# Down-projection weights of layer 1 on GpSimd's queue, two tiles ahead in four buffers, and the first tile's weight sums placed in the out-projection

## The chip, the cores and the metric

One core of one Trainium2 chip runs the whole program. Its engines are TensorE (PE, with its weight loads as PEld), VectorE (DVE, `V` in the code), ScalarE (ACT, `S`), GpSimd (POOL, `G`) and SyncE (SP), which here only issues DMAs. The metric is the device time of one execution in microseconds (us).

## The reference

A backbone block of two layers on 1024 latent tokens (and 256 context tokens) of width 1024. Layer 0 mixes by Fourier groups and windowed attention, layer 1 by neighbourhood attention; each layer ends with a SwiGLU feed-forward part of inner width 2816. The part that matters is layer 1's end:

```python
x = x + g1 * o                                     # o = mixer output @ w_out
h = _rms(x, norm2_g[i]) * (1.0 + sc2) + sh2
x = x + g2 * _swiglu(h, ffn_w_gate[i], ffn_w_up[i], ffn_w_down[i])

def _swiglu(h, wg, wu, wd):
    return (jax.nn.silu(h @ wg) * (h @ wu)) @ wd
```

All inputs are float32.

## The kernel before

Every float32 product is made of three matmuls on split operands: a number is hi + lo, hi its cast to the PE's float32 format, lo the rest, and hi·hi + lo·hi + hi·lo is summed in PSUM (`mm3`, L74 to L76; L76 is the last of a group). So each weight tile that arrives raw from memory must first be cast (ACT) and subtracted (DVE or POOL). `parts_of` does it for four 128x128 blocks at a time: the cast to w_hi at L1239, and the subtraction to w_lo at L1244, on POOL straight from w_hi, on DVE from a copy of w_hi in PSUM (`pmisc`, L1243).

Layer 1 ends with three loops. `out_proj1` runs once for each half (`ci` = 0, 1) of 512 tokens, over eight output tiles of 128 columns in falling order; it prepares the next tile's weights ahead, advances a norm's generator (`own`: `norm1s`) by one step and a second (`side`) by three. `norm1s` writes h in eight pieces of 128x512 (nrm_h). For the first half they go to `combine`, which makes the sums s_sum on POOL and splits them into c_hi and c_lo; the second half's pieces are stored to memory (h_d) and read back later as h_in.

Then, for each half, the feed-forward part walks 22 tiles (`NF`) of 128 inner columns. `gate_up1(f)` computes gate and up of tile f with a seven-product scheme for 2x2 block matrices: the gate and up weights (w_gate, w_up, 128x1024 each, loaded by SP at L1232 into a ring of four buffers w_raw) are the four blocks b11, b21, b12, b22, and POOL forms the sums t1 to t4 (L1328, L1329, L1333, L1337). `product7` makes one product p_ps of 12 matmuls 128x256; there are three PSUM buffers for these. ACT copies the first product to p (L1331), DVE adds the others up, ACT applies Silu, and act_hi (L1358) and act_lo (L1359) are the split result. The blocks b21 and b22 have their w_lo made on POOL, the other five on DVE.

`down_weights1(f)` loads tile f's down weights in two parts (wd_raw, 128x512, by SP at L1373, two buffers), casts them on ACT (L1374) and subtracts on POOL (L1375) into the "room": the buffers of the out-projection's inputs h_out[1], so both the hi and the lo parts are called h_hi or h_lo by the name of the buffer, depending on the pair. `down1` multiplies two tiles' results by their down weights: eight d_ps groups of six matmuls 128x512, each added to x by DVE (L1384). It runs for tiles f − 2 and f − 1 after the products of each even f, so the period of the loop is two tiles, called a pair below. The first four of the eight groups read the first part of each tile's room, the last four the second part.

A scheduler orders each engine's instructions from the program order and its own estimate of when they can run; the engines then keep that order, and each engine's queue is in order. That holds for SP's DMA issues too. Semaphores carry the waits between engines.

Of the kernel before, what the change touches and what calls it, by code (L numbers as in the profile page):

```python
# [9 lines left out]
F32 = mybir.dt.float32  # L10
F32R = mybir.dt.float32r
AF = mybir.ActivationFunctionType
ALU = mybir.AluOpType
# [3 lines left out]
P = 128  # L17
# [10 lines left out]
NF = DFF // P  # L28
# [35 lines left out]
def build(tc, io):  # L64
    nc = tc.nc
    V, S, G, TE = nc.vector, nc.scalar, nc.gpsimd, nc.tensor
    pools = Pools(tc)

    def fl(ap):
        return ap.bitcast(F32)  # L70

    def mm3(out, lh, ll, rh, rl, first, last):

        TE.matmul(out, lh, rh, start=first, stop=False)  # L74
        TE.matmul(out, lh, rl, start=False, stop=False)  # L75
        TE.matmul(out, ll, rh, start=False, stop=last)  # L76
# [35 lines left out]
    def vec(l, which):  # L112
        return mod[l][:, which * KT:(which + 1) * KT, :]
# [36 lines left out]
    def advance(steps, n):  # L150

        for _ in range(n):
            if next(steps, steps) is steps:
                return
# [35 lines left out]
    wk, wk_cm = pools.open("wk0", bufs=2, side="right")  # L190
# [158 lines left out]
    for c in range(T // CH):  # L349
        h_hi, h_lo = hs[c]  # L350

        for u in range(CH // P):
# [34 lines left out]
            for i, h0, nh in ((0, 0, 8), (1, 8, 2)):  # L387
                src = pqf[:, h0 * HD:(h0 + nh) * HD]
# [83 lines left out]
    for half in range(2):  # L472
# [5 lines left out]
        for gg in range(2):  # L478
# [3 lines left out]
            for i0, parts in ((0, (0, 4)), (2, (1, 2)), (4, (3,))):  # L482
# [8 lines left out]
                n = len(parts)  # L491
                src = ps[:, 0:n].rearrange("p n r l -> p r n l")
# [18 lines left out]
    g = fp.tile([P, 2, 512], F32, name="fg", tag="fa")  # L511
# [6 lines left out]
    for grp in range(4):  # L518
# [5 lines left out]
        src = ps.rearrange("p n r l -> p r n l")  # L524
# [699 lines left out]
    wk, wk_cm = pools.open("wk1")  # L1224
# [5 lines left out]
    def raw_weights(src):  # L1230
        raw = wr.tile([P, KT, P], F32, name="w_raw")
        nc.sync.dma_start(raw, src)  # L1232
        return raw

    def parts_of(src, eng=V):


        hi, lo = (ww.tile([P, 4, P], F32R, name=n) for n in ("w_hi", "w_lo"))
        S.copy(hi, src)  # L1239
        first = fl(hi)  # L1240
        if eng is V:
            first = ph.tile([P, 512], F32, name="pmisc").rearrange("p (k n) -> p k n", n=P)
            S.copy(first, fl(hi))  # L1243
        eng.tensor_tensor(lo, src, first, ALU.subtract)  # L1244
        return hi, lo

    def out_weights(dt):
        raw = raw_weights(io["w_out1"][dt])
        old = wr.tile([P, SEQ], F32, name="x_old", tag="w_raw")
        nc.sync.dma_start(old, x_d[:, dt])  # L1250
        return [parts_of(raw[:, i:i + 4]) for i in (0, 4)], old

    def out_proj1(ci, ready, own, side=iter(()), then=lambda: None):

        h_hi, h_lo = h_out[ci]
        for dt in reversed(range(KT)):
            ws, old = ready
            ready = out_weights(dt - 1) if dt else then()
            ps = pd.tile([P, 512], F32, name="d_ps")
            for k in range(KT):  # L1260
                hi, lo = ws[k // 4]
                mm3(ps, hi[:, k % 4], lo[:, k % 4], h_hi[:, k], h_lo[:, k], k == 0, k == KT - 1)
            cols = slice(ci * 32, ci * 32 + 32)
            V.scalar_tensor_tensor(x[:, dt, ci * 512:ci * 512 + 512].rearrange("p (c r) -> p c r", r=GH),
                                   ps.rearrange("p (c r) -> p c r", r=GH), vec(1, 2)[:, dt, 0:1],
                                   old.rearrange("p (r c) -> p r c", c=GW)[:, :, cols].rearrange("p r c -> p c r"),
                                   ALU.mult, ALU.add)
            advance(own, 1)
            advance(side, 3)
        return ready  # L1270

    def norm1s(ci, adder, done):


        ts = slice(ci * 512, ci * 512 + 512)
        ss = wk.tile([P, 512], F32, name="nrm_ss")
        for i, k in enumerate(reversed(range(KT))):
            if i == 0:
                S.activation(ss, x[:, k, ts], AF.Square)
            else:  # L1280
                sq = wk.tile([P, 512], F32, name="nrm_sq", tag="t", bufs=4)
                S.activation(sq, x[:, k, ts], AF.Square)
                adder.tensor_tensor(ss, ss, sq, ALU.add)
            yield
        for r in norm_rstd(ss, 512, wk, ph):
            yield
        for i in range(4):
            both = []
            for k in (i, i + 4):
                t = wk.tile([P, 512], F32, name="nrm_t", tag="t", bufs=4)  # L1290
                V.scalar_tensor_tensor(t, x[:, k, ts], nA[3][:, k, 0:1], r, ALU.mult, ALU.mult)
                h = wk.tile([P, 512], F32, name="nrm_h", bufs=2)
                S.activation(h, t, AF.Identity, bias=vec(1, 3)[:, k, 0:1], scale=1.0)
                both.append(h)
                yield
            done(i, *both)
            yield
# [19 lines left out]
            mm3(ps, w[0][:, k], w[1][:, k], c_hi[:, slot, k], c_lo[:, slot, k], k == 0, k == 3)  # L1317
        return ps

    def gate_up1(f, side=iter(())):  # L1320
        g, u = raw_weights(io["w_gate"][1, f]), raw_weights(io["w_up"][1, f])
        b11, b21, b12, b22 = g[:, 0:4], g[:, 4:8], u[:, 0:4], u[:, 4:8]
        t1, t2, t3, t4 = (wk.tile([P, 4, P], F32, name=n, tag="t", bufs=4) for n in ("t1", "t2", "t3", "t4"))
        p1, u2, u3, sg = (wk.tile([P, HT], F32, name=n) for n in ("p1", "u2", "u3", "sg"))
        av = wk.tile([P, 2, HT], F32, name="av", bufs=2)
        hi, lo = (wk.tile([P, 512], F32R, name=n, bufs=4) for n in ("act_hi", "act_lo"))
        w = parts_of(b11)
        G.tensor_tensor(t1, b12, b11, ALU.subtract)  # L1328
        G.tensor_tensor(t2, b22, t1, ALU.subtract)  # L1329
        ps = product7(w, 0)  # L1330
        S.copy(p1, ps)  # L1331
        w = parts_of(t2)
        G.tensor_tensor(t3, b22, b12, ALU.subtract)  # L1333
        ps = product7(w, 4)
        V.tensor_tensor(u2, ps, p1, ALU.add)
        w = parts_of(t3)
        G.tensor_tensor(t4, t2, b21, ALU.subtract)  # L1337
        ps = product7(w, 5)
        V.tensor_tensor(u3, ps, u2, ALU.add)
        w = parts_of(t1)  # L1340
        ps = product7(w, 3)
        V.tensor_tensor(av[:, 1], ps, u3, ALU.add)
        V.tensor_tensor(u2, ps, u2, ALU.add)
        w = parts_of(t4)
        ps = product7(w, 2)
        V.tensor_tensor(u3, u3, ps, ALU.subtract)
        S.activation(u3, u3, AF.Silu)
        w = parts_of(b21, G)
        ps = product7(w, 1)
        V.tensor_tensor(av[:, 1], av[:, 1], u3, ALU.mult)  # L1350
        V.tensor_tensor(sg, ps, p1, ALU.add)
        S.activation(sg, sg, AF.Silu)
        w = parts_of(b22, G)
        ps = product7(w, 6)
        V.tensor_tensor(u2, ps, u2, ALU.add)
        V.tensor_tensor(av[:, 0], u2, sg, ALU.mult)
        avf = av.rearrange("p a n -> p (a n)")
        S.copy(hi, avf)  # L1358
        V.tensor_tensor(lo, avf, fl(hi), ALU.subtract)  # L1359
        advance(side, 2)  # L1360
        return hi, lo
# [6 lines left out]
    def down_weights1(f):  # L1368

        w_in = w_room[f // 2 % 2]  # L1370
        for h in range(2):
            raw = wk.tile([P, 4, P], F32, name="wd_raw", bufs=2)
            nc.sync.dma_start(raw, io["w_down"][1, f][:, 4 * h:4 * h + 4])  # L1373
            S.copy(w_in[:, f % 2, h, 0], raw)  # L1374
            G.tensor_tensor(w_in[:, f % 2, h, 1], raw, fl(w_in[:, f % 2, h, 0]), ALU.subtract)  # L1375

# [16 lines left out]
    own0 = norm1s(0, G, combine)  # L1393
    ready = out_proj1(0, out_weights(KT - 1), own0, then=lambda: out_weights(KT - 1))
# [2 lines left out]
    c_hi = cc.tile([P, 7, 4, HT], F32R, name="c_hi")  # L1397
    c_lo = cc.tile([P, 7, 4, HT], F32R, name="c_lo")
    own1 = norm1s(1, V, keep)
    out_proj1(1, ready, own1, own0)  # L1400
    advance(own0, 99)
    for ci in range(2):
        acts = {}
        for f in range(NF):
            if f:
                down_weights1(f - 1)
            acts[f] = gate_up1(f, own1 if f else iter(()))
            if f % 2 == 0 and 2 <= f < NF - 2:
                down1(ci, (f - 2, f - 1), [acts.pop(f - 2), acts.pop(f - 1)], False)
        down_weights1(NF - 1)  # L1410

        h_in = []
        for i in range(4 if ci == 0 else 0):
            h_in.append(wr.tile([P, 2, 512], F32, name="h_in", tag="w_raw"))
            for n in range(2):
                nc.sync.dma_start(h_in[i][:, n], h_d[:, i + 4 * n])

        def amid(dt):
            if dt % 4 == 1 and h_in:
                h = h_in.pop(0)  # L1420
                combine(3 - len(h_in), h[:, 0], h[:, 1], tags=("t", "t"))

        for f in (NF - 4, NF - 2):
            down1(ci, (f, f + 1), [acts.pop(f), acts.pop(f + 1)], f == NF - 2, amid)
# [113 lines left out]
```

## Time and profile before

| | |
|---|---|
| runs | 3011.53, 3016.84, 3020.38 us; median 3016.84 |
| profiled execution | 3014.64 us; its span, first to last instruction, 3012.9 us |
| instructions | 44371 |
| mean granted TensorE clock | 0.976 |
| busy | PE 95%, PEld 79%, DVE 51%, ACT 40%, POOL 27% of the span |
| out-projection's end and feed-forward of layer 1 | from about 2195 us to the end, 3012.9 us |

In profile rows a time is followed by a duration, the engine and the line. "PE p_ps L74 <- ACT p L1331: 29.2, 8, 5.2" means that PE, about to run line 74, waited for the instruction of ACT at line 1331: 29.2 us in total, 8 times, 5.2 at most. In the rows of single instructions, a bracket at the end holds the idle time of the engine just before and what ended it; "x4" means four neighbouring instructions told as one row. "SPq" is SP issuing DMAs: a long duration there means that later issues of the row waited for buffers.

### The profile page before, as it was taken

Reading aid. Unit: us, or ns where it says so; the run is one execution under the profiler, and the core shown is the slowest. Engines: PE = TensorE matmul, PEld = TensorE weight load, DVE = VectorE, ACT = ScalarE, POOL = GpSimd, SP = SyncE. Lnnn points to the kernel's source line nnn. Section 1 sums busy time; section 2 is a strip of 40 time slices with the busy share of each in tenths; the row PEclk is TensorE's granted clock in tenths of the full one; section 3 lists DMA queues with packets and bytes.
Section 4 is the critical chain, followed back from the end, with each engine's and each line's share of the span. In section 5 each row is a group of like instructions: output and inputs, shape, how many; then the busy total and the mean of one; then the engine's idle time right before and its main releaser. Section 6 shows DMA issues by size and latency. Waiting matters only on the chain. (4 is left out here: it accounts for less than half of the span.)

```text
span 3012.9 us, 44371 instructions
## 1 busy us (share of the span) xinstructions
PE 2848.3 (95%) x16874; PEld 2383.4 (79%) x16874; DVE 1550.6 (51%) x3084; ACT 1200.7 (40%) x2390; POOL 809.7 (27%) x826
## 2 busy tenths in 40 slices
PE   7989999999999999999899999999989898889899
PEld 5876768888888888888767887777778888788888
DVE  5775553632323333333673343665566566755566
ACT  4445552411111111111452223666665555655553
POOL 0112322000000000000310003553266555755553
PEclk9989999999999999999999999999989999999999
DMA  7236563111111110110244338773533222422221
GB/s 271 101 99 244 211 227 116 49 43 49 36 35 35 43 39 32 42 42 30 74 128 121 99 102 203 177 172 93 168 120 121 91 85 85 140 85 85 85 85 64
DMA packets 137701, 310.59 MB, mean 103 GB/s; under 512 B 11504, under 2 KB 69360, under 8 KB 130448
## 3 DMA queue, kind: packets, MB, share of 16 engines
q1 hardware_dynamic: 129056, 288.80, 30.5%
q0 software_dynamic: 1952, 8.32, 1.0%
q10 hardware_dynamic: 6480, 10.63, 0.9%
q8 instruction: 134, 2.20, 0.3%
q14 instruction: 79, 0.65, 0.1%
HBM read 264.58 MB, written 43.12 MB: 102 GB/s over the span
## 5 line engine op out<-in xcount | busy, mean ns | idle before, releaser
L74 PE MATMUL p_ps<-c_hi,w_hi 128*128 128x256 f32 x1232 | 364.5, 296 | 75.9 <-ACT p L1331 58.1
L76 PE MATMUL p_ps<-c_hi,w_lo 128*128 128x256 f32 x1232 | 358.7, 292 | 6.6 <-DVE w_lo L1244 3.4
L75 PE MATMUL p_ps<-c_lo,w_hi 128*128 128x256 f32 x1232 | 358.7, 291 | 0.0
L74 PEld LDWEIGHTS p_ps<-c_hi,w_hi 128*128 128x128 f32 x1232 | 249.2, 202 | 84.5 <-ACT p L1331 62.5
L810 POOL TENSOR_TENSOR nrm_ss<-nrm_ss,nrm_sq 128x512 f32<-128x512 f32 (+1 forms) x31 | 39.3, 1269 | 1013.1 <-PE d_ps L76 935.7
L775 ACT CAST w_hi<-w_raw 128x1024 fp32r<-128x1024 f32 x106 | 110.2, 1049 | 482.5 <-PE d_ps L75 270.5
L76 PEld LDWEIGHTS p_ps<-c_hi,w_lo 128*128 128x128 f32 x1232 | 248.3, 202 | 8.1 <-DVE w_lo L1244 4.1
L75 PEld LDWEIGHTS p_ps<-c_lo,w_hi 128*128 128x128 f32 x1232 | 249.8, 203 | 0.9
L580 POOL TENSOR_SCALAR pr<-pr,st 128x640 f32<-128x640 f32 (+2 forms) x208 | 156.1, 751 | 267.2 <-DVE st L579 176.9
L878 DVE SCALAR_TENSOR_TENSOR x<-d_ps,mod,x 128x512 f32<-128x512 f32 (+1 forms) x240 | 157.6, 661 | 125.3 <-PE d_ps L76 125.3
L776 DVE TENSOR_TENSOR w_lo<-w_raw,w_hi 128x1024 fp32r<-128x1024 f32 x102 | 124.1, 1223 | 184.7 <-ACT w_hi L775 182.3
L862 DVE TENSOR_TENSOR sg<-sg,u_ps 128x512 f32<-128x512 f32 (+1 forms) x66 | 39.5, 599 | 320.0 <-PE u_ps L76 320.0
L74 PE MATMUL d_ps<-act_hi,w_hi 128*128 128x512 f32 (+1 forms) x528 | 189.3, 359 | 3.4 <-DVE x L878 3.4
L75 PE MATMUL d_ps<-act_lo,w_hi 128*128 128x512 f32 (+1 forms) x528 | 189.2, 358 | 1.3 <-DVE act_lo L864 1.3
L76 PE MATMUL d_ps<-act_hi,w_lo 128*128 128x512 f32 (+1 forms) x528 | 189.3, 358 | 0.0
L74 PE MATMUL u_ps<-o_hi,w_hi 128*128 128x512 f32 (+1 forms) x528 | 188.3, 357 | 0.0
L75 PE MATMUL u_ps<-o_lo,w_hi 128*128 128x512 f32 (+1 forms) x528 | 188.3, 357 | 0.0
L76 PE MATMUL u_ps<-o_hi,w_lo 128*128 128x512 f32 (+1 forms) x528 | 188.3, 357 | 0.0
L74 PE MATMUL g_ps<-o_hi,w_hi 128*128 128x512 f32 (+1 forms) x528 | 188.3, 357 | 0.0
L75 PE MATMUL g_ps<-o_lo,w_hi 128*128 128x512 f32 (+1 forms) x528 | 188.2, 357 | 0.0
L76 PE MATMUL g_ps<-o_hi,w_lo 128*128 128x512 f32 (+1 forms) x528 | 188.2, 357 | 0.0
L574 ACT ACTIVATE pr<-sm,st 128x640 f32<-128x640 f32 (+4 forms) x208 | 162.7, 782 | 31.1 <-POOL sm L563 22.3
(321 smaller groups left out, 7437.4 us busy)
## 6 DMA issues: line engine op xcount, KB each, us to landing
ada_w<-ada_w SPq DMA_DIRECT2D x48, 1024.0 KB, 4.9
w_raw<-w_gate SPq DMA_DIRECT2D x66, 512.0 KB, 3.5
w_raw<-w_up SPq DMA_DIRECT2D x66, 512.0 KB, 3.9
wd_raw<-w_down SPq DMA_DIRECT2D x88, 256.0 KB, 2.8
k<-k_d SPq DMA_DIRECT2D x28, 640.0 KB, 10.0
w_raw<-w_out SPq DMA_DIRECT2D x32, 512.0 KB, 3.6
w_raw<-w_in SPq DMA_DIRECT2D x24, 512.0 KB, 4.0
w_raw<-w_down SPq DMA_DIRECT2D x22, 512.0 KB, 3.5
```

Of the source, the lines that this page charges most:

```text
L74: TE.matmul(out, lh, rh, start=first, stop=False)
L75: TE.matmul(out, lh, rl, start=False, stop=False)
L76: TE.matmul(out, ll, rh, start=False, stop=last)
L574: S.activation(self.pr[:, :n], self.sm[:, :n], AF.Exp, bias=st[:, 0:1], scale=-1.0, accum_out=st[:, 1:2])
L580: G.tensor_scalar(self.pr[:, :n], self.pr[:, :n], st[:, 3:4], 0.0, ALU.mult, ALU.add)
L775: S.copy(hi, raw)
L776: eng.tensor_tensor(lo, raw, fl(hi), ALU.subtract)
L810: adder(i).tensor_tensor(ss, ss, sq, ALU.add)
L862: V.tensor_tensor(sg[:, :n], sg[:, :n], u_ps[:, :n], ALU.mult)
L878: V.scalar_tensor_tensor(xs, self.shaped(ps[:, :n]), vec(l, 5)[:, dt, v:v + 1], xs, ALU.mult, ALU.add)
```

## The change

Five things change. The down weights are loaded by GpSimd's queue instead of SP's, their ring has four buffers and shares them with nrm_h (which had two of its own), and `down_weights1` is called two tiles ahead of the tile's use in program order. `out_weights` passes `past=False`, so that DVE subtracts from w_hi itself and ACT's copy to PSUM is left out in the out-projection. The side generator goes two steps per tile instead of three. And the loads and the first two sums of the first feed-forward tile are called at the last tile of the second half's `out_proj1`.

```diff
@@ -1232,13 +1232,13 @@
         nc.sync.dma_start(raw, src)
         return raw
 
-    def parts_of(src, eng=V):
+    def parts_of(src, eng=V, past=True):
 
 
         hi, lo = (ww.tile([P, 4, P], F32R, name=n) for n in ("w_hi", "w_lo"))
         S.copy(hi, src)
         first = fl(hi)
-        if eng is V:
+        if eng is V and past:
             first = ph.tile([P, 512], F32, name="pmisc").rearrange("p (k n) -> p k n", n=P)
             S.copy(first, fl(hi))
         eng.tensor_tensor(lo, src, first, ALU.subtract)
@@ -1248,7 +1248,7 @@
         raw = raw_weights(io["w_out1"][dt])
         old = wr.tile([P, SEQ], F32, name="x_old", tag="w_raw")
         nc.sync.dma_start(old, x_d[:, dt])
-        return [parts_of(raw[:, i:i + 4]) for i in (0, 4)], old
+        return [parts_of(raw[:, i:i + 4], past=False) for i in (0, 4)], old
 
     def out_proj1(ci, ready, own, side=iter(()), then=lambda: None):
 
@@ -1266,7 +1266,7 @@
                                    old.rearrange("p (r c) -> p r c", c=GW)[:, :, cols].rearrange("p r c -> p c r"),
                                    ALU.mult, ALU.add)
             advance(own, 1)
-            advance(side, 3)
+            advance(side, 2)
         return ready
 
     def norm1s(ci, adder, done):
@@ -1289,7 +1289,7 @@
             for k in (i, i + 4):
                 t = wk.tile([P, 512], F32, name="nrm_t", tag="t", bufs=4)
                 V.scalar_tensor_tensor(t, x[:, k, ts], nA[3][:, k, 0:1], r, ALU.mult, ALU.mult)
-                h = wk.tile([P, 512], F32, name="nrm_h", bufs=2)
+                h = wk.tile([P, 512], F32, name="nrm_h", tag="wd", bufs=4)
                 S.activation(h, t, AF.Identity, bias=vec(1, 3)[:, k, 0:1], scale=1.0)
                 both.append(h)
                 yield
@@ -1317,16 +1317,24 @@
             mm3(ps, w[0][:, k], w[1][:, k], c_hi[:, slot, k], c_lo[:, slot, k], k == 0, k == 3)
         return ps
 
-    def gate_up1(f, side=iter(())):
-        g, u = raw_weights(io["w_gate"][1, f]), raw_weights(io["w_up"][1, f])
+    def load_gate_up(f):
+        return [raw_weights(io[w][1, f]) for w in ("w_gate", "w_up")]
+
+    def first_sums(g, u):
+        t1, t2 = (wk.tile([P, 4, P], F32, name=n, tag="t", bufs=4) for n in ("t1", "t2"))
+        G.tensor_tensor(t1, u[:, 0:4], g[:, 0:4], ALU.subtract)
+        G.tensor_tensor(t2, u[:, 4:8], t1, ALU.subtract)
+        return t1, t2
+
+    def gate_up1(f, side=iter(()), raws=None):
+        g, u = raws[:2] if raws else load_gate_up(f)
         b11, b21, b12, b22 = g[:, 0:4], g[:, 4:8], u[:, 0:4], u[:, 4:8]
-        t1, t2, t3, t4 = (wk.tile([P, 4, P], F32, name=n, tag="t", bufs=4) for n in ("t1", "t2", "t3", "t4"))
+        t1, t2 = raws[2:] if raws else first_sums(g, u)
+        t3, t4 = (wk.tile([P, 4, P], F32, name=n, tag="t", bufs=4) for n in ("t3", "t4"))
         p1, u2, u3, sg = (wk.tile([P, HT], F32, name=n) for n in ("p1", "u2", "u3", "sg"))
         av = wk.tile([P, 2, HT], F32, name="av", bufs=2)
         hi, lo = (wk.tile([P, 512], F32R, name=n, bufs=4) for n in ("act_hi", "act_lo"))
         w = parts_of(b11)
-        G.tensor_tensor(t1, b12, b11, ALU.subtract)
-        G.tensor_tensor(t2, b22, t1, ALU.subtract)
         ps = product7(w, 0)
         S.copy(p1, ps)
         w = parts_of(t2)
@@ -1369,8 +1377,8 @@
 
         w_in = w_room[f // 2 % 2]
         for h in range(2):
-            raw = wk.tile([P, 4, P], F32, name="wd_raw", bufs=2)
-            nc.sync.dma_start(raw, io["w_down"][1, f][:, 4 * h:4 * h + 4])
+            raw = wk.tile([P, 4, P], F32, name="wd_raw", tag="wd", bufs=4)
+            G.dma_start(raw, io["w_down"][1, f][:, 4 * h:4 * h + 4])
             S.copy(w_in[:, f % 2, h, 0], raw)
             G.tensor_tensor(w_in[:, f % 2, h, 1], raw, fl(w_in[:, f % 2, h, 0]), ALU.subtract)
 
@@ -1397,17 +1405,22 @@
     c_hi = cc.tile([P, 7, 4, HT], F32R, name="c_hi")
     c_lo = cc.tile([P, 7, 4, HT], F32R, name="c_lo")
     own1 = norm1s(1, V, keep)
-    out_proj1(1, ready, own1, own0)
+    def first_tile():
+        g, u = load_gate_up(0)
+        return g, u, *first_sums(g, u)
+
+    ready = out_proj1(1, ready, own1, own0, then=first_tile)
     advance(own0, 99)
     for ci in range(2):
         acts = {}
         for f in range(NF):
-            if f:
-                down_weights1(f - 1)
-            acts[f] = gate_up1(f, own1 if f else iter(()))
+            if f < NF - 1:
+                down_weights1(f + 1 if f else 0)
+            if f == 0:
+                down_weights1(1)
+            acts[f] = gate_up1(f, own1 if f else iter(()), ready if f + ci == 0 else None)
             if f % 2 == 0 and 2 <= f < NF - 2:
                 down1(ci, (f - 2, f - 1), [acts.pop(f - 2), acts.pop(f - 1)], False)
-        down_weights1(NF - 1)
 
         h_in = []
         for i in range(4 if ci == 0 else 0):
```

In the changed kernel the lines move by eight or so: t1 is L1325, t2 L1326, t3 L1341, t4 L1345, the copy to p L1339, act_hi L1366, the wd load L1381, its cast L1382 and its subtraction L1383.

First place: POOL in the steady loop, one pair from the second tile's w_lo of the tile before. w_lo are subtractions for b21 and b22, h_lo the subtractions of down weights, t the sums. Before:

```order
L1329 TENSOR_TENSOR t_21683<-w_raw,t_21682 128x512
L1333 TENSOR_TENSOR t_21684<-w_raw 128x512
L1337 TENSOR_TENSOR t_21685<-t_21683,w_raw 128x512
L1244 TENSOR_TENSOR w_lo<-w_raw,w_hi 128x512
L1375 TENSOR_TENSOR h_lo<-wd_raw,h_lo 128x512 x4
L1244 TENSOR_TENSOR w_lo<-w_raw,w_hi 128x512
L1328 TENSOR_TENSOR t_21916<-w_raw 128x512
```

The same engine and place after (the names of the room's buffers alternate by pair, so h_hi stands here):

```order
L1345 TENSOR_TENSOR t_22851<-t_22847,w_raw 128x512
L1244 TENSOR_TENSOR w_lo<-w_raw,w_hi 128x512
L1383 TENSOR_TENSOR h_hi<-wd_raw,h_hi 128x512
L1381 DMA wd_raw<-w_down 128x512
L1383 TENSOR_TENSOR h_hi<-wd_raw,h_hi 128x512
L1381 DMA wd_raw<-w_down 128x512
L1383 TENSOR_TENSOR h_hi<-wd_raw,h_hi 128x512
L1381 DMA wd_raw<-w_down 128x512
L1383 TENSOR_TENSOR h_hi<-wd_raw,h_hi 128x512
L1381 DMA wd_raw<-w_down 128x512
L1244 TENSOR_TENSOR w_lo<-w_raw,w_hi 128x512
L1325 TENSOR_TENSOR t_23008<-w_raw 128x512
```

The four subtractions stay between the w_lo of b21 and that of b22, and a DMA issue now stands behind each. On SP the rows `w_down 128x512 x4` are gone, and only gate and up loads are left in this loop.

Second place: POOL where the second half's out-projection ends and the first tile of the feed-forward part begins. s_sum are the last sums of `combine` for the first half. Before:

```order
L1307 TENSOR_TENSOR s_sum<-nrm_h 128x256
L1305 TENSOR_TENSOR s_sum<-nrm_h 128x256
L1306 TENSOR_TENSOR s_sum<-s_sum,nrm_h 128x256
L1308 TENSOR_TENSOR s_sum<-nrm_h,s_sum 128x256
L1375 TENSOR_TENSOR h_hi<-wd_raw,h_hi 128x512 x3
L1328 TENSOR_TENSOR t_18860<-w_raw 128x512
L1375 TENSOR_TENSOR h_hi<-wd_raw,h_hi 128x512
L1329 TENSOR_TENSOR t_18861<-w_raw,t_18860 128x512
L1333 TENSOR_TENSOR t_18862<-w_raw 128x512
```

After:

```order
L1307 TENSOR_TENSOR s_sum<-nrm_h 128x256
L1325 TENSOR_TENSOR t_18767<-w_raw 128x512
L1381 DMA wd_raw<-w_down 128x512
L1305 TENSOR_TENSOR s_sum<-nrm_h 128x256
L1326 TENSOR_TENSOR t_18768<-w_raw,t_18767 128x512
L1306 TENSOR_TENSOR s_sum<-s_sum,nrm_h 128x256
L1381 DMA wd_raw<-w_down 128x512
L1308 TENSOR_TENSOR s_sum<-nrm_h,s_sum 128x256
L1381 DMA wd_raw<-w_down 128x512 x2
L1341 TENSOR_TENSOR t_18816<-w_raw 128x512
L1383 TENSOR_TENSOR h_hi<-wd_raw,h_hi 128x512
```

t1 and t2 (here t_18767 and t_18768) have moved ahead of the first subtractions of down weights and into the last group of s_sum, with the first wd issues among them.

## The prediction

> **What bounds the kernel now.** I read the page's busy times first, then busy times by stretch, then the waits of one steady stretch, then one period of the loop engine by engine. The page says that TensorE is nearly always busy and POOL a quarter of the time:
>
> ```profile
> PE 2848.3 (95%) x16874; PEld 2383.4 (79%) x16874; DVE 1550.6 (51%) x3084; ACT 1200.7 (40%) x2390; POOL 809.7 (27%) x826
> ```
>
> That is a mean over the program. The diff touches layer 1's feed-forward stage, from 2195 us to the end, and by stretch it reads (columns: length, PE, PEld, DVE, ACT, POOL, then clock, DMA share, GB/s):
>
> ```profile
> 2358.90:2543.20 184.30, 164.79 (x1081) 151.96 (x1081) 112.63 (x190) 95.83 (x180) 106.81 (x80) 0.93 0.27 86
> 2658.70:2953.60 294.90, 265.57 (x1729) 244.46 (x1728) 180.62 (x304) 153.65 (x288) 170.81 (x128) 0.92 0.26 86
> 2195.50:2246.00 50.50, 38.72 (x280) 36.52 (x279) 27.55 (x50) 33.63 (x62) 35.53 (x28) 0.86 0.37 122
> ```
>
> The first two rows hold 5 and 8 periods of two weight tiles each (a pair): 184.30/5 and 294.90/8 are both 36.86 us. The loop is regular, PE isn't full in it, and its clock is granted at 0.92. The waits of the 8 pairs:
>
> ```profile
> ACT h_hi L1374 <- DMA wd_raw<-w_down: 47.4, 8, 9.8
> POOL t L1328 <- DMA w_raw<-w_up: 43.5, 10, 4.8
> PE p_ps L74 <- ACT p L1331: 29.2, 8, 5.2
> POOL h_hi L1375 <- ACT h_hi L1374: 24.9, 8, 4.7
> POOL h_lo L1375 <- ACT h_lo L1374: 20.6, 7, 4.2
> POOL t L1328 <- DVE w_lo L1244: 17.8, 4, 4.6
> POOL h_lo L1375 <- PE p_ps L75: 4.4, 1, 4.4
> ```
>
> PE waits once a pair, 29.2/8 = 3.65 us, for ACT's copy of a product. That copy stands in ACT's queue behind the four casts of down weights, and those wait for their loads. One pair in time:
>
> ```profile
> 2432.02 10.73 SPq L1373 DMA_DIRECT2D wd_raw<-w_down  x4
> 2435.73 1.14 ACT L1374 CAST h_lo<-wd_raw 128x512 fp32r<-128x512 f32 x2 [8.22 <-DMA wd_raw<-w_down]
> 2440.41 0.62 ACT L1374 CAST h_lo<-wd_raw 128x512 fp32r<-128x512 f32 x1 [3.54 <-DMA wd_raw<-w_down]
> 2441.36 0.58 PE L74 MATMUL p_ps<-c_hi,w_hi 128*128 128x256 f32 x1 [3.59 <-ACT p L1331]
> 2442.35 1.29 POOL L1244 TENSOR_TENSOR w_lo<-w_raw,w_hi 128x512 fp32r<-128x512 f32 x1
> 2443.66 0.33 SPq L1232 DMA_DIRECT2D w_raw<-w_up  x1
> 2447.61 1.30 POOL L1328 TENSOR_TENSOR t<-w_raw 128x512 f32<-128x512 f32 x1 [3.97 <-DMA w_raw<-w_up]
> ```
>
> With two buffers, a load starts only when a subtraction on POOL has freed one, so cast, subtraction and load take turns over 10.73 us. PE's stall is one victim. POOL is the other: its subtractions wait for the casts, and behind them stands w_lo of b22, whose end frees the buffer that the next w_up load needs (2443.66 follows 2442.35 + 1.29), and t1 waits for that load. So POOL and SP make a closed loop: w_lo, w_up load, four sums t, w_lo, and again.
>
> Two floors follow. **POOL's**: its cluster waits are 24.9 + 20.6 + 4.4 = 49.9 us in 8 pairs, 6.24 a pair; without them the loop takes 36.86 − 6.24 = 30.6 us. The waits of t1 after w_lo (43.5 + 17.8 = 61.3 us in 14, 4.4 each; those with a DVE name follow w_lo by the same time, so I count them as load time) stay in it. **PE's**:
>
> ```profile
> 2433.52 0.28 PE L74 MATMUL p_ps<-c_hi,w_hi 128*128 128x256 f32 x1
> 2437.49 0.28 PE L76 MATMUL p_ps<-c_hi,w_lo 128*128 128x256 f32 x1
> 2429.52 0.75 DVE L1384 SCALAR_TENSOR_TENSOR x<-d_ps,mod,x 128x512 f32<-128x512 f32 x1 [0.45 <-PE d_ps L76]
> 2433.72 0.75 DVE L1384 SCALAR_TENSOR_TENSOR x<-d_ps,mod,x 128x512 f32<-128x512 f32 x1 [0.65 <-PE d_ps L76]
> 2441.74 0.41 PE L75 MATMUL p_ps<-c_lo,w_hi 128*128 128x256 f32 x1
> 2441.95 0.41 PE L76 MATMUL p_ps<-c_hi,w_lo 128*128 128x256 f32 x1
> 2477.74 0.58 PE L74 MATMUL p_ps<-c_hi,w_hi 128*128 128x256 f32 x1 [2.80 <-ACT p L1331]
> ```
>
> From the first row to the second are 35 steps of 0.1134 us; 168 product matmuls make 19.1. Three down tiles end 4.20 us apart, 1.40 each; eight make 11.2. Together 30.3 us. The rest of 36.86 is the stall (3.65) and 2.9 for what follows it: steps of 0.21 instead of 0.113 us, half the clock.
>
> **The change, part by part.** *Loads to POOL's queue, two tiles ahead, four buffers.* SP loses four issues a pair; POOL gets four, each behind the subtraction that frees its buffer and waiting for nothing else. No POOL issue is in this stage before; elsewhere:
>
> ```profile
> 1804.31 2.34 POOL L1109 DMA_DIRECT2D k<-k_d  x4
> 142.81 0.71 POOL L370 DMA_DIRECT2D tw<-twiddle  x1
> 1818.41 0.53 POOL L1109 DMA_DIRECT2D v<-v_d  x1 [2.44 <-DMA k<-k_d]
> ```
>
> So 0.53 to 0.71 us each; I take 0.65, near the upper row, as each also waits for the operation ahead of it: 4 × 0.65 = 2.6 a pair, all on POOL, with t1, w_lo and the next load queued behind. POOL's loop becomes 30.6 + 2.6 = 33.2 us. The loads now land a pair early, so the casts wait for PE alone, for the down products that read their room (half the room is free after the fourth of eight, the rest after the last). I add 0.2 for the third cast, which comes just behind the last down product: 33.4, against PE's 30.3. POOL is the bound and PE's surplus of 3.1 us becomes a wait for POOL's w_lo of b21. Saving 36.86 − 33.4 = 3.46 a pair, 13 pairs: −45. Bounds: 30.3 a pair (PE's floor, −85) and 36.86 (0).
>
> The Trainium skill speaks against this part: its page "SBUF — State Buffer", section "SBUF: two separate sides", says that a DMA issued from GpSimd's queue has its descriptors written by GpSimd, which is locked out while VectorE holds the port pair that they share, and gives about 620 ns for one such DMA alone and about 3100 ns beside a VectorE copy. If all four issues met that, they would be some 10 us a pair dearer (an estimate from that page, 4 × 2.5), and the change a loss. The rows above agree with the 620; no row of this case shows the 3100.
>
> *First tile's sums amid the out-projection.* The next rows show the seam:
>
> ```profile
> 2186.45 0.73 POOL L1308 TENSOR_TENSOR s_sum<-nrm_h,s_sum 128x256 f32<-128x256 f32 x1
> 2191.29 0.33 SPq L1232 DMA_DIRECT2D w_raw<-w_up  x1
> 2199.84 1.72 POOL L1328 TENSOR_TENSOR t<-w_raw 128x512 f32<-128x512 f32 x1
> 2202.73 1.26 POOL L1329 TENSOR_TENSOR t<-w_raw,t 128x512 f32<-128x512 f32 x1
> 2204.02 0.62 ACT L1239 CAST w_hi<-t 128x512 fp32r<-128x512 f32 x1 [4.07 <-POOL t L1329]
> 2204.70 0.58 PE L74 MATMUL p_ps<-c_hi,w_hi 128*128 128x256 f32 x1 [7.62 <-ACT w_hi L1239]
> ```
>
> PE stalls 7.62 us for t2, which POOL makes at 2202.7 because t1 and t2 stand behind down-weight subtractions. Put ahead of those, t1 can start when the w_up load lands (issued at 2191.29, so at about 2195.3 by the 3.97 us of the pair above). By the new order the last s_sum group, done at 2187.2 before, now stands behind t1 and among the issues: t1 to 2196.9, an issue, s_sum, t2, s_sum to about 2201 (their rows' 0.7 to 1.3 us each), then the split of that sum on ACT and DVE. So the second product can begin near 2202 instead of 2204.7. I take −3, with a little of the half clock after the stall (0.86 in that stretch); bounds +3 (s_sum later still, through the slower side generator) and −12 (the whole idle time of PE in 2195 to 2246, 50.5 − 38.7).
>
> *The out-projection's ACT copies.* 33 copies go, and DVE's subtraction reads two SBUF operands:
>
> ```profile
> L1243 ACT COPY pmisc<-w_hi 128x512 f32<-128x512 f32 x33 | 18.6, 582 | 0.1
> PE d_ps L74 <- ACT w_hi L1239: 1.9, 2, 1.0
> PE d_ps L76 <- DVE w_lo L1244: 2.0, 3, 1.0
> ```
>
> The copies are hidden under PE but for these 3.9 us. I take −2, bounds −4 and +3 (DVE slower by such reads, and the sums' two issues beside the other half's norm).
>
> *Four buffers shared with the norm's h, and side work two steps at a time.* In the first three or four pairs h is written and stored from the same ring, so some issues on POOL wait for a store, with t1 behind them. PE waits little there today. I take +2, bounds −6 and +12. At the boundary between the two token halves POOL has eight subtractions and issues together: −2, bounds −5 and +10. The last tile's loads no longer come late:
>
> ```profile
> 2960.69 0.38 PE L74 MATMUL p_ps<-c_hi,w_hi 128*128 128x256 f32 x1 [2.81 <-ACT p L1331]
> ```
>
> That wait goes: −2, bounds −3 and 0.
>
> Sum: −45 − 3 − 2 + 2 − 2 − 2 = −52. The profiled execution took 3014.64 us, so 2962.6; the median of the runs stands 2.2 above it: 2965.
>
> **The rivals.** *PE becomes the bound* (B). If POOL's issues overlap its arithmetic, the loop is 30.6 and PE's 30.3 to 31.5 rules: 13 × 5.9 = 77 saved there, some 7 elsewhere, about 2933. For it speaks little: neighbouring POOL operations overlap by only 0.03 us here (2451.56 + 1.48 is 2453.04, and the next starts at 2453.01):
>
> ```profile
> 2451.56 1.48 POOL L1337 TENSOR_TENSOR t<-t,w_raw 128x512 f32<-128x512 f32 x1
> 2453.01 3.00 POOL L1244 TENSOR_TENSOR w_lo<-w_raw,w_hi 128x512 fp32r<-128x512 f32 x2
> ```
>
> *The half clock comes back* (C). If PE's new wait of some 3 us is again followed by half speed, the two products behind it take up to 2.7 us more, the down products end later, and the third subtraction on POOL waits for them: 35 to 36 a pair, saving 11 to 24; with 7 elsewhere about 2990 (2986 to 2999). For it: the row at 2477.74, where 2.80 us of waiting was enough. Against: POOL's issues lie between, and take up about 1.5 us of that delay. The Trainium skill, page "TensorE: Matmul & The Clock Gate", section "Part 1: The HAM clock gate", puts the drop after an idle window of some 3.4 us, by which a wait of 3 us would be free; the row at 2477.74 says otherwise.
>
> *Nothing changes* (D). The casts could wait as long for PE's last down product as they did for loads. Against: that product ends about 2433.5, and PE's stall began at 2437.7, when the fourth cast still had 2.7 us to go. About 3015.
>
> *Slower* (E). POOL's issue costs more here than in the quoted rows, since POOL must share something with a DVE that is busy 61% of this stretch (180.62/294.90). If POOL could issue only while DVE is idle, 0.65 us would become 0.65/0.39 = 1.7; and the loop loses what it gained at (36.86 − 30.6)/4 = 1.57 us each. If one issue took what four take in the row at 1804.31, 2.34 us, the pair would take 30.6 + 9.4 = 40.0: 13 × 3.1 = 40 more, less the 7 saved elsewhere, about 3050. Against: beside the cluster DVE mostly runs x at L1384, 0.75 us in every 1.40, so an issue would wait for the end of one such operation at most. The rule of the page "SBUF — State Buffer" in the Trainium skill, quoted above, is this mechanism.
>
> **How the numbers follow.** My forecast 0.56 (2943 to 2980), B 0.13, C 0.16, D 0.06, E 0.09. The range goes from B's lower part, 2924, to C's upper, 2997; outside lie D, E and a little of B and C, about 0.19. A difference under 0.3% (9 us) isn't told from none here. Faster: forecast, B and most of C, 0.84. Same: D and C's rest, 0.07. Slower: E, 0.09.
>
> **What the profile would show.** In the steady stretch: the pair at 33.4 us; POOL's L1381 rows of about 0.6 us between subtractions; no wait of ACT's casts for wd loads, but short ones for PE's d_ps; PE waiting some 3 us a pair for POOL's w_lo instead of ACT's p; t1's waits for w_up unchanged at 4.4. At the seam, a PE wait near 5 us instead of 7.62. I am wrong if L1381 rows take over 1 us, if the casts end over 2 us after the last down product, or if the first four pairs grow.

## The result and the profile after

| | before | after |
|---|---|---|
| runs, median | 3017.55 us (4 runs) | 2964.86 us (2961.52 to 2966.66, 4 runs) |
| ratio | | 0.9827, 95% interval 0.9809 to 0.9844 |
| span of the profiled execution | 3012.9 us | 2962.5 us |
| mean granted clock | 0.976 | 0.984 |

The change makes the kernel 1.7% faster; 2965 was forecast. The page after, for the line shown of before:

```profile
span 2962.5 us, 44248 instructions
PE 2820.2 (95%) x16874; PEld 2361.8 (80%) x16874; DVE 1555.9 (53%) x3084; ACT 1196.2 (40%) x2358; POOL 847.3 (29%) x914
```

Busy time by stretch, the same 5 and 8 steady pairs, and the seam (columns as before; the clock stands third from the end):

```profile
2363.44:2528.92 165.48, 156.77 (x1083) 144.43 (x1082) 107.29 (x190) 99.36 (x180) 114.85 (x101) 0.98 0.30 96
2643.83:2908.08 264.25, 249.95 (x1731) 230.33 (x1730) 173.73 (x304) 158.69 (x288) 182.78 (x159) 0.98 0.30 95
2195.50:2246.00 50.50, 39.14 (x270) 36.74 (x271) 36.30 (x52) 36.62 (x67) 41.46 (x40) 0.84 0.37 125
```

A pair takes 165.48/5 = 33.1 and 264.25/8 = 33.0 us instead of 36.86. PE's busy time in the seam's row hardly differs from before (39.14 for 38.72 us). The waits of the 8 pairs after:

```profile
POOL t L1325 <- DMA w_raw<-w_up: 70.6, 16, 5.7
ACT h_hi L1382 <- PE d_ps L75: 32.6, 9, 4.3
PE p_ps L76 <- POOL w_lo L1244: 14.3, 10, 2.0
POOL wd_raw L1381 <- POOL h_lo L1383: 3.9, 13, 0.3
```

ACT's casts now wait for PE's down products and no longer for wd loads; POOL has no wait for a cast left; t1 waits for w_up as it did (70.6/16 = 4.4 us). PE's wait for p is gone, and one for POOL's w_lo of b21 has come, 14.3/8 = 1.8 us a pair. POOL's timeline through one cluster, and the same point one pair later:

```profile
2705.49 1.31 POOL L1244 TENSOR_TENSOR w_lo<-w_raw,w_hi 128x512 fp32r<-128x512 f32 x1
2706.73 1.31 POOL L1383 TENSOR_TENSOR h_hi<-wd_raw,h_hi 128x512 fp32r<-128x512 f32 x1
2708.34 0.55 POOL L1381 DMA_DIRECT2D wd_raw<-w_down  x1 [0.30 <-POOL h_hi L1383]
2708.92 1.30 POOL L1383 TENSOR_TENSOR h_hi<-wd_raw,h_hi 128x512 fp32r<-128x512 f32 x1
...
2715.45 1.30 POOL L1244 TENSOR_TENSOR w_lo<-w_raw,w_hi 128x512 fp32r<-128x512 f32 x1
...
2738.32 1.31 POOL L1244 TENSOR_TENSOR w_lo<-w_raw,w_hi 128x512 fp32r<-128x512 f32 x1
```

This pair is 2738.32 − 2705.49 = 32.8 us of POOL's time, without an idle stretch but t1's two load waits and the 0.30 ahead of each issue. The cluster of four subtractions and four issues takes 2715.45 − 2706.73 = 8.72 us; four subtractions in a row take 5.0 (5.04 in a row of the variant with SP's queue, below). So an issue costs (8.72 − 5.0)/4 = 0.93 us: 0.55 for itself, 0.30 of idle time between the end of the subtraction ahead and the issue, and the small overlap lost.

Where the 50.4 us of span went, from the end of one pair's last DVE addition (L1384, L1392) to that of a later one, and in the first two rows at PE's first p_ps matmul:

| stretch | before | after | difference | forecast |
|---|---|---|---|---|
| start to the first product of the feed-forward part | 2195.5 | 2190.2 | −5.3 | −2 |
| that product to the first pair's end (seam) | 61.8 | 64.8 | +3.0 | −3 |
| pairs 2 to 4 | 102.6 | 108.4 | +5.8 | +2 |
| 5 + 8 steady pairs | 184.3 + 294.9 | 165.5 + 264.3 | −49.5 | −45 |
| between the halves | 115.5 | 114.9 | −0.6 | −2 |
| last pairs to the end | 58.3 | 54.4 | −3.9 | −2 |

### The profile page after: what moved, and what is told of

The parts are those of the page before. It is cut to its first block, busy times and chain, and to the rows that moved or that the text cites. A ratio compares the mean times of both kernels' runs of the same rounds, so it can differ in the third digit from the quotient of the medians.

```text
span 2962.5 us, 44248 instructions
## 1 busy us (share of the span) xinstructions
PE 2820.2 (95%) x16874; PEld 2361.8 (80%) x16874; DVE 1555.9 (53%) x3084; ACT 1196.2 (40%) x2358; POOL 847.3 (29%) x914
## 5 line engine op out<-in xcount | busy, mean ns | idle before, releaser
L76 PE MATMUL p_ps<-c_hi,w_lo 128*128 128x256 f32 x1232 | 352.3, 286 | 39.1 <-POOL w_lo L1244 31.6
L74 PE MATMUL p_ps<-c_hi,w_hi 128*128 128x256 f32 x1232 | 350.7, 285 | 22.2 <-DVE u L1347 5.6
L75 PE MATMUL p_ps<-c_lo,w_hi 128*128 128x256 f32 x1232 | 349.4, 284 | 0.0
L76 PEld LDWEIGHTS p_ps<-c_hi,w_lo 128*128 128x128 f32 x1232 | 239.7, 195 | 45.6 <-POOL w_lo L1244 37.1
L74 PEld LDWEIGHTS p_ps<-c_hi,w_hi 128*128 128x128 f32 x1232 | 239.8, 195 | 25.2 <-DVE u L1347 5.8
L75 PEld LDWEIGHTS p_ps<-c_lo,w_hi 128*128 128x128 f32 x1232 | 239.9, 195 | 0.9
```

## The experiments

The theory after the result: POOL's loop sets the pair, about 29.1 us of its own work and of load time and 0.93 us for every issue in it; PE's 30.3 would rule if POOL's were shorter. Its rivals are that PE's or the loads' side sets it, that the place of the queue doesn't matter, or that the look-ahead is what counts. "Steady pair" is the length of the second eight pairs over 8.

| kernel | median us | ratio to before, 95% | steady pair us |
|---|---|---|---|
| changed kernel | 2964.86 | 0.9827 (0.9809 to 0.9844) | 33.0 |
| e1: SP's queue, four buffers, ahead | 2911.3 | 0.9637 (0.9622 to 0.9651) | 30.5 |
| e2: loads split in two issues | 2998.15 | 0.9926 (0.991 to 0.9943) | 34.1 |
| e3: before with GpSimd's queue only | 3004.89 | 0.9948 (0.9932 to 0.9964) | 35.1 |
| e4: the loads' part alone | 2970.6 | 0.9834 (0.982 to 0.9849) | 33.0 |
| e5: e1 without the look-ahead | 2910.85 | 0.9643 (0.9625 to 0.966) | 30.5 |
| e6: SP's queue, two buffers, ahead | 3019.81 | 0.9997 (0.9987 to 1.0006) | 36.6 |
| e7: ACT's queue | 2938.21 | 0.9726 (0.9711 to 0.9741) | 32.6 |
| e8: two of four subtractions on DVE | 2939.08 | 0.973 (0.9711 to 0.975) | 30.9 |
| e9: before with four buffers only | 2912.53 | 0.9638 (0.9625 to 0.9651) | 30.5 |
| e10: the rest of the change without the loads | 3025.97 | 1.0008 (0.9999 to 1.0017) | 36.7 |

### e1: SP's queue again

```diff
-            G.dma_start(raw, io["w_down"][1, f][:, 4 * h:4 * h + 4])
+            nc.sync.dma_start(raw, io["w_down"][1, f][:, 4 * h:4 * h + 4])
```

> The down weights are loaded by SP again; the four buffers, the two tiles ahead and the rest of the change stay. Theory (POOL's loop sets the steady pair: 29.1 us of sums, subtractions and gate/up load time, plus about 0.93 us for each of four issues that stand between its subtractions): without the issues POOL needs 29.1, so PE's 30.3 to 31.3 rules, and 13 pairs save 1.6 to 2.6 each against the changed kernel: 2931 to 2944 us. Rival 1 (PE or the look-ahead alone decides, the queue is indifferent): 2960 to 2970. Rival 2 (SP's queue was the trouble: wd issues that wait there hold up gate and up loads): over 2975, casts waiting for wd loads again.

Measured: 2911.3 us, 53.6 less than the changed kernel and 20 below the theory's range. Busy time in the 5 and 8 steady pairs:

```profile
2353.00:2505.50 152.50, 152.43 (x1083) 140.40 (x1082) 111.59 (x191) 97.69 (x180) 104.94 (x80) 1.00 0.32 102
2611.25:2855.63 244.38, 243.05 (x1731) 225.12 (x1730) 172.32 (x304) 156.48 (x288) 168.32 (x130) 1.00 0.33 104
```

PE's only wait in the 8 pairs, and the first of POOL's:

```profile
PE p_ps L76 <- POOL w_lo L1244: 1.3, 2, 1.0
POOL t L1325 <- DMA w_raw<-w_up: 38.6, 8, 5.2
```

POOL's four subtractions in its timeline, without issues between them:

```profile
2700.42 5.04 POOL L1383 TENSOR_TENSOR h_lo<-wd_raw,h_lo 128x512 fp32r<-128x512 f32 x4
```

PE is busy 243.05 of 244.38 us at full clock, so the pair of 30.5 is nearly its floor (243.05/8 = 30.4). But POOL has no slack either, and here the theory's 29.1 fails. POOL's only waits are the 16 of t1 (74.8 us with those under DVE names), and each ends 0.2 us after its w_up load has landed, a load that is issued 0.03 us after POOL's w_lo. With 168.32 us of work they make (168.32 + 74.8)/8 = 30.4 a pair: both engines are full, and this run can't tell which of the two sets the 30.5.

The two profiled spans differ by 51.8 us. The steady pairs give 429.7 − 396.9 = 32.8 of them, and nearly all the rest lies outside: pairs 2 to 4 take 98.3 us (108.4 in the changed kernel), the stretch between the halves 105.7 (114.9). So POOL's issues cost there as well, which the theory's range had left out.

### e2: twice as many issues

```diff
-            G.dma_start(raw, io["w_down"][1, f][:, 4 * h:4 * h + 4])
+            for j in (0, 2):
+                G.dma_start(raw[:, j:j + 2], io["w_down"][1, f][:, 4 * h + j:4 * h + j + 2])
```

> The changed kernel with each down-weight load issued as two of 128x256: eight issues a pair, of which seven stand between POOL's subtractions and the w_lo of b22 and one behind it. Theory: three more issues in the loop, 0.57 us each where they follow another issue, up to 0.93 behind a subtraction: 1.7 to 2.8 a pair, steady pair 34.5 to 35.7, total 2987 to 3001 us. Rival (POOL's issue is hidden and PE or the landing of loads sets the pair): 2960 to 2970.

Measured: 2998.15 us, in the theory's range; the pair is 34.1, a little under it. POOL's timeline, from a cluster's first subtraction to the row behind its last:

```profile
2758.74 1.29 POOL L1384 TENSOR_TENSOR h_lo<-wd_raw,h_lo 128x512 fp32r<-128x512 f32 x1
...
2762.14 1.61 POOL L1382 DMA_DIRECT2D wd_raw<-w_down  x3
...
2768.30 1.29 POOL L1244 TENSOR_TENSOR w_lo<-w_raw,w_hi 128x512 fp32r<-128x512 f32 x1
2769.52 0.55 POOL L1382 DMA_DIRECT2D wd_raw<-w_down  x1
```

The cluster takes 9.56 instead of 8.72 us: three more issues at 0.55 are 1.65, but two of the 0.30 gaps are gone (1.05 is left; 0.84 was measured): an issue whose buffer was freed one subtraction earlier follows at once. The eighth stands behind w_lo, in the wait for w_up, and costs little there. The pair grows with the issues in the loop: POOL's loop is the bound, and the price is per issue, not per byte.

### e3: the queue alone

```diff
-            nc.sync.dma_start(raw, io["w_down"][1, f][:, 4 * h:4 * h + 4])
+            G.dma_start(raw, io["w_down"][1, f][:, 4 * h:4 * h + 4])
```

This is the kernel before but for that line.

> The kernel before, with only the queue of the down-weight loads changed to GpSimd's: two buffers, no look-ahead, SP and ACT as before. By the order three issues and three subtractions stand ahead of the w_lo of b22, the fourth subtraction behind it. Theory: the third load is issued behind the first subtraction and lands 2.9 us later, so POOL waits some 2 us for it; 29.1 + 3 x 0.93 + 2.2 = 34.1, less 1.2 for the subtraction that moved into the wait for w_up: 32.9 to 34.5 a pair, 2966 to 2986 us. Rival (the two buffers alone make the pair 36.9, and issues come on top): 3015 to 3050.

Measured: 3004.89 us, a pair of 35.1. Both missed: better than the rival, worse than the theory. POOL's cluster in the timeline:

```profile
2761.20 0.55 POOL L1373 DMA_DIRECT2D wd_raw<-w_down  x1 [0.30 <-POOL h_lo L1375]
2765.44 1.28 POOL L1375 TENSOR_TENSOR h_lo<-wd_raw,h_lo 128x512 fp32r<-128x512 f32 x1 [3.68 <-ACT h_lo L1374]
```

Three of the waits in its 8 steady pairs:

```profile
ACT h_lo L1374 <- DMA wd_raw<-w_down: 37.4, 7, 8.4
DVE w_lo L1244 <- ACT pmisc L1243: 49.2, 44, 6.1
PE p_ps L74 <- DVE u L1339: 22.6, 8, 4.5
```

With two buffers the wait for the load comes at the second subtraction, 3.68 us, where I had assumed two loads in hand: its cast needs the load that is issued behind the first subtraction (e6 shows why). And ACT's queue, held by the last cast, is late with the copies behind it, for which DVE and then PE wait.

### e4: the loads' part alone

```diff
-        return [parts_of(raw[:, i:i + 4], past=False) for i in (0, 4)], old
+        return [parts_of(raw[:, i:i + 4], past=True) for i in (0, 4)], old
...
-            advance(side, 2)
+            advance(side, 3)
...
-    ready = out_proj1(1, ready, own1, own0, then=first_tile)
+    out_proj1(1, ready, own1, own0)
```

(The first tile then makes its own loads and sums.)

> Only the loads' part of the change: GpSimd's queue, two tiles ahead, four buffers shared with nrm_h. The out-projection keeps ACT's copies and three side steps, and the first tile's sums stay where they were. Theory: the steady pair stays at 32.9 and this part carries nearly all: 2962 to 2972 us. Rival (the seam and the out-projection carry a good share): 2985 or more.

Measured: 2970.6 us and the same pair. The loads carry the result; by the medians the other parts add 5.7 us beside them, by the ratios (0.9834 and 0.9827, intervals that overlap) 2.

### e5: no look-ahead

```diff
-            if f < NF - 1:
-                down_weights1(f + 1 if f else 0)
-            if f == 0:
-                down_weights1(1)
+            if f:
+                down_weights1(f - 1)
...
+        down_weights1(NF - 1)
```

Applied to e1.

> As the variant with SP's queue and four buffers (2911 us, steady pair 30.5), but each tile's loads stand again where they stood before in program order, not two tiles ahead. SP's order in the loop keeps gate, four wd loads, up. Theory (the buffers carry the gain: a load may start as soon as one is free, and four free ones are a pair's worth): pair 30.5, 2908 to 2920 us. Rival (the program order ahead carries it): casts wait for wd loads, pair 33 to 36.9, 2945 to 3010.

Measured: 2910.85 us against e1's 2911.3. In program order the loads stand two tiles later, but on SP they stand at the same place, between a gate and an up load, and each starts as soon as its buffer is free. On SP's queue the look-ahead of the source adds nothing; with GpSimd's it was not tried alone.

### e6: two buffers

```diff
-                h = wk.tile([P, 512], F32, name="nrm_h", tag="wd", bufs=4)
+                h = wk.tile([P, 512], F32, name="nrm_h", bufs=2)
...
-            raw = wk.tile([P, 4, P], F32, name="wd_raw", tag="wd", bufs=4)
+            raw = wk.tile([P, 4, P], F32, name="wd_raw", bufs=2)
```

Applied to e1.

> As the variant with SP's queue, two tiles ahead, but with two buffers of their own for wd and two for nrm_h, as before. Theory: two loads are there when the cluster starts; the third is issued behind the first subtraction, lands 2.9 us later and is cast in 0.6, so the cluster of four subtractions takes 7.4 instead of 5.0 us: POOL's loop 29.1 + 2.4 = 31.5, 2918 to 2930 us. Rival (two buffers are the whole trouble of before, whatever the program order): pair 35 to 36.9, 2975 or more.

Measured: 3019.81 us, a ratio of 0.9997: the rival. SP's, ACT's and POOL's timelines:

```profile
2736.94 0.33 SPq L1381 DMA_DIRECT2D wd_raw<-w_down  x1
2740.25 0.33 SPq L1381 DMA_DIRECT2D wd_raw<-w_down  x1
...
2761.19 0.62 ACT L1382 CAST h_lo<-wd_raw 128x512 fp32r<-128x512 f32 x1 [2.52 <-PE d_ps L75]
2765.61 1.31 POOL L1383 TENSOR_TENSOR h_lo<-wd_raw,h_lo 128x512 fp32r<-128x512 f32 x1
2766.95 10.28 SPq L1381 DMA_DIRECT2D wd_raw<-w_down  x4
2770.39 1.14 ACT L1382 CAST h_lo<-wd_raw 128x512 fp32r<-128x512 f32 x2 [8.58 <-PE p_ps L75]
2774.88 0.62 ACT L1382 CAST h_lo<-wd_raw 128x512 fp32r<-128x512 f32 x1 [3.35 <-DMA wd_raw<-w_down]
```

Two loads are there when the cluster starts, as I said: those issued at 2736.94 and 2740.25 land within 2.7 us, and no buffer stays empty, since each load is issued some 0.03 us after the subtraction that frees its buffer (2765.61 + 1.31 = 2766.92, then 2766.95). What fails is the next step, that the third load is the first to be waited for. The second cast waits until 2770.39, when the load of 2766.95 has landed (3.4 us); the third follows at once, with no further wd load landed, so its load had been in hand. The code makes a reason likely: two buffers hold the first and the second part of one tile, while the casts take the first parts of both tiles first, because the first four down products free those places of the room. So the second cast needs the buffer of the first, and the cluster takes its two turns of load, cast and subtraction as before (10.28 us; 10.73 in the kernel before, where the casts come in the same way). This order of the casts is read from the times and the code, not from a run that changes it. With four buffers all four parts are loaded a pair early, whatever their order.

### e7: ACT's queue

```diff
-            G.dma_start(raw, io["w_down"][1, f][:, 4 * h:4 * h + 4])
+            nc.scalar.dma_start(raw, io["w_down"][1, f][:, 4 * h:4 * h + 4])
```

> The changed kernel with the wd loads issued by ACT's queue, two behind each two casts, ahead of the copy to p. Theory: POOL's loop is free of issues (29.1), and ACT's issues wait for POOL's subtractions, the last of which ends some 0.7 us before PE needs p: pair 30.5 to 31.5, 2911 to 2928 us. Rival (p is held up as before, PE waits for ACT): pair 33 or more, PE waiting for p, 2945 or more.

Measured: 2938.21 us, between the two, a pair of 32.6. ACT's copy and POOL's next step in the timeline:

```profile
2689.92 0.37 ACT L1339 COPY p<-p_ps 128x256 f32<-128x256 f32 x1 [2.49 <-POOL h_hi L1383]
2690.89 1.29 POOL L1244 TENSOR_TENSOR w_lo<-w_raw,w_hi 128x512 fp32r<-128x512 f32 x1 [1.38 <-ACT w_hi L1239]
```

PE's wait for p in the 8 pairs:

```profile
PE p_ps L74 <- ACT p L1339: 4.0, 7, 1.6
```

ACT's issues stand ahead of p and wait for POOL's last subtraction; the cast of b22 stands behind p, and POOL waits 1.38 us for it. So the loop gets a new link, POOL to ACT to POOL, of 11.0/8 = 1.4 us a pair, and POOL waits nearly as long again, 9.0/8 = 1.1, for the third cast, which stands behind ACT's first two issues. The margin of 0.7 us that I gave p held nearly (PE waits 4.0 us in 7); what I left out were the casts behind the issues.

### e8: two subtractions on DVE

```diff
-            G.tensor_tensor(w_in[:, f % 2, h, 1], raw, fl(w_in[:, f % 2, h, 0]), ALU.subtract)
+            (V if h else G).tensor_tensor(w_in[:, f % 2, h, 1], raw, fl(w_in[:, f % 2, h, 0]), ALU.subtract)
```

> The changed kernel (GpSimd's queue kept) with the second half's subtraction of each tile's down weights moved from POOL to DVE: two of four a pair. Theory (POOL's loop is the bound): two subtractions of 1.25 and two waits of 0.3 leave the loop, 33.0 to 29.9, so PE's 30.5 rules: 13 x 2.4 = 31 us less than the changed kernel, 2925 to 2940 us. Rival (PE waits for something else, or DVE, 66% busy there, becomes late): 2958 or more.

Measured: 2939.08 us, in the theory's range; the pair is 30.9, and of PE's wait for POOL 1.7 us in 8 pairs are left. Busy time of those pairs, then the wait:

```profile
2634.51:2881.85 247.34, 245.58 (x1741) 226.66 (x1740) 186.22 (x322) 157.88 (x290) 164.77 (x145) 1.00 0.32 103
```

```profile
PE p_ps L76 <- POOL w_lo L1244: 1.7, 4, 0.7
```

The queue is GpSimd's still, so it was POOL's time, and not the down-weight loads or their landing, that set the changed kernel's pair.

### e9: four buffers and nothing else

```diff
-                h = wk.tile([P, 512], F32, name="nrm_h", bufs=2)
+                h = wk.tile([P, 512], F32, name="nrm_h", tag="wd", bufs=4)
...
-            raw = wk.tile([P, 4, P], F32, name="wd_raw", bufs=2)
+            raw = wk.tile([P, 4, P], F32, name="wd_raw", tag="wd", bufs=4)
```

Applied to the kernel before.

> The kernel before with nothing changed but the ring: wd_raw and nrm_h share four buffers instead of two each. SP's queue, the program order, ACT's copies and the first tile's sums stay as before. Theory (the four buffers carry the gain): steady pair 30.5, total 2910 to 2922 us, the upper end if the seam and the out-projection are worth the 6 us by which the loads alone fell short of the whole change. Rival (the other parts hold a share that only shows without POOL's issues): 2930 or more.

Measured: 2912.53 us; the ratio 0.9638 is e1's and e5's within the intervals. Two lines do what the variant with all other parts does.

### e10: everything but the loads

The changed kernel with e5's and e6's edits and SP's queue: what is left are the out-projection without ACT's copies, two side steps, and the first tile's sums.

> The kernel before with everything of the change but the loads: out-projection without ACT's copies, two side steps, the first tile's sums ahead; wd loads on SP with two buffers each for wd and nrm_h, in the old program order. Theory: the steady pair stays at 36.9, the seam gains 3 to 8: 3009 to 3019 us beside a before of 3020. Rival (these parts carry more): under 3005.

Measured: 3025.97 us beside 3022.34, ratio 1.0008 (0.9999 to 1.0017). The 3 to 8 us that I expected of these parts did not come: they move nothing that can be measured in the whole.

## Why the prediction was right, step by step

**The steady loop.** Right in mechanism, and e2 and e8 show it: POOL's loop was the hidden bound behind PE's visible stall, and with the cluster waits gone it stays the bound, by its issues. The size also came out, 33.1 for 33.4. Without issues (e1) the pair is 30.5, where 30.6 was estimated for POOL's loop, and the four issues add 33.0 − 30.5 = 2.5, where 2.6 was estimated. That 2.5 is partly luck, as it is a net. In its cluster an issue was sized 0.65 and costs 0.93: the 0.1 that I allowed for waiting on the operation ahead is 0.30, and an overlap is lost too. That is 1.1 us too little a pair. Against it the rest of POOL's loop is shorter than in e1: the waits for w_up are 70.6/8 = 8.8 for 74.8/8 = 9.35, and its arithmetic is (182.78 − 30 × 0.553)/8 = 20.8 us for 168.32/8 = 21.0 (30 of the issues fall in that stretch). The 0.2 for the third cast never came: POOL waits for no cast in the 8 pairs.

The arithmetic before was longer still, 170.81/8 = 21.4. The trace tells where: 24 of its 128 operations in the 8 pairs last over 1.4 us, and 9 of 128 after; the median of the others is 1.29 and 1.30. Of the long ones 23 and 9 begin while DVE runs act_lo (L1359, L1367) or av (L1356, L1364). That such an overlap makes them longer was not tried.

**PE's new wait** was placed right, on w_lo of b21, and is 14.3/8 = 1.8 us for some 3. Most of the rest is half clock, which still follows now and then (0.98): PE is busy 249.95 us in the 8 pairs and 243.05 in e1, at full clock, which makes 0.9 a pair. Rival C did not come about in size: a pair of 33.0 leaves no room for its 35 to 36. B was realised only where POOL has no issues (e1, e5, e9), and E would have needed 1.57 us an issue.

**The lock on descriptor writing.** All 88 issues of the changed kernel last about the same, with DVE busy 66% of the steady stretch (173.73/264.25); the row gives least, median and most in ns:

```profile
L1381 POOL DMA_DIRECT2D wd_raw<-w_down x88: 536/553/590, 2193.0 to 2880.9; - x88
```

So the rule of the Trainium skill's page "SBUF — State Buffer", section "SBUF: two separate sides", priced 620 ns alone and 3100 beside a VectorE copy, did not bite: POOL's 0.55 us agrees with the first. But no run here tests the second, since DVE runs no copy in this stage: its 779 operations from 2192 to 2882 us are tensor_tensor and scalar_tensor_tensor. The prediction counted a busy DVE as the condition, where the page names a copy.

**First pairs.** Forecast +2, measured +5.8, and the step named the wrong cause. I blamed the ring shared with the norm's h. e1 and e9 share it too and take 98.3 and 96.4 us, less than before; e1 differs from the changed kernel in the queue alone, so it is the issues on POOL. The wait for a store that I expected is there once, 2.7 us:

```profile
POOL wd_raw L1381 <- DMA h_d<-nrm_h: 2.7, 1, 2.7
```

**The seam and the out-projection.** Forecast −2 and −3, measured −5.3 and +3.0: a gain that was sized too small and one that became a loss. PE reaches the first product 5.3 us earlier; the first row here is before, the next three after:

```profile
2195.50 0.28 PE L74 MATMUL p_ps<-c_hi,w_hi 128*128 128x256 f32 x1
2190.21 0.28 PE L74 MATMUL p_ps<-c_hi,w_hi 128*128 128x256 f32 x1
PE d_ps L74 <- ACT w_hi L1239: 1.0, 1, 1.0
PE d_ps L76 <- DVE w_lo L1244: 0.3, 1, 0.3
```

Of the 3.9 us of waits in the out-projection 1.3 are left, and the two stretches of half clock that followed them before (mean clock 0.97 from 2090 us to the first product) are gone (1.00). Whether the copies or the side steps did it was not tried apart. The rows of PE, POOL and DVE at the seam after, and as the last row the last sum's split before:

```profile
2196.22 0.58 PE L74 MATMUL p_ps<-c_hi,w_hi 128*128 128x256 f32 x1 [4.14 <-ACT w_hi L1239]
2202.18 0.58 PE L76 MATMUL p_ps<-c_hi,w_lo 128*128 128x256 f32 x1 [5.16 <-DVE w_lo L1244]
2191.24 1.77 POOL L1325 TENSOR_TENSOR t<-w_raw 128x512 f32<-128x512 f32 x1 [2.55 <-DMA w_raw<-w_up]
2194.25 1.27 POOL L1326 TENSOR_TENSOR t<-w_raw,t 128x512 f32<-128x512 f32 x1
2196.71 0.74 POOL L1308 TENSOR_TENSOR s_sum<-nrm_h,s_sum 128x256 f32<-128x256 f32 x1
2198.93 2.60 DVE L1312 TENSOR_TENSOR c_lo<-s_sum,c_hi 128x512 fp32r<-128x512 f32 x1
2201.45 0.68 DVE L1244 TENSOR_TENSOR w_lo<-t,pmisc 128x512 fp32r<-128x512 f32 x1
2187.87 0.69 DVE L1312 TENSOR_TENSOR c_lo<-s_sum,c_hi 128x512 fp32r<-128x512 f32 x1
```

t2 is indeed early, by 8 us, since the w_up load came 3.5 us earlier as well. But the last s_sum, done at 2187.2 before, ends at 2197.4 behind t1, t2 and the first issues; its split occupies DVE until 2201.5, and the w_lo of t2 stands behind it there. That split takes 2.60 us where it took 0.69 before; why was not tried. PE's longest stall of 7.62 us became two, 4.14 and 5.16, and its waits from 2195.5 to 2246 us add up to 14.6 for 11.9. The prediction saw the late sum and priced its effect on PE at a gain of 3; it was a wait turned into another, and a loss. e10, with the same edits, shows both parts again: its first product begins 325.2 us after PE's 10000th matmul, which lies ahead of all that changes (329.3 before, 324.5 after), and its first pair ends 67.4 us later (61.8 before). So nothing is left in the whole.

**Between the halves and the end**: −0.6 and −3.9 for −2 and −2.

What the prediction didn't ask is which part of the edit gains. The buffers are worth 110 us by themselves (e9); GpSimd's queue takes 54 of these back (e1 against the changed kernel); the look-ahead (on SP's queue) and the rest are worth nothing that shows. The fastest versions are e9, with two lines changed, and e1 and e5, which equal it within their intervals.

## What to carry to other kernels

When an engine stalls behind a load, count first how many loads are in hand and which of them the next operation needs: here two more buffers did all, and neither another queue nor an earlier place in program order did. Before an issue is moved to a compute engine, add up that engine's loop; an engine 27% busy over the program was the bound of the loop that it was asked to serve. And an operation put forward on an in-order queue puts back whatever it passes: ask who waits for that.

## What the runs showed that was not expected

An issue on POOL behind the operation that frees its buffer costs 0.93 us in its cluster, not its own 0.55: 0.30 of idle time lies between that operation's end and the issue, while neighbouring arithmetic runs on without a gap (5.04 us for four subtractions of 1.29). And two loads in hand can be the wrong two: in e6 both buffers were full from 2743 us on, and the second cast still waited until 2770, for a load into the buffer that the first was to free.
